# Differential attention: loads and operands of q and k earlier, and three small steps in other forms

## The chip, the cores and the metric

The kernel runs on one core of one Trainium2 chip. The metric is the time of one execution on the device in microseconds (us), the median of several runs. The names of the engines: TensorE (PE, with its weight loads shown as PEld), VectorE (DVE), ScalarE (ACT), GpSimd (POOL) and SyncE (SP), which here only issues transfers.

## What is computed

One step of a two-layer decoder trunk: a gated-linear-attention layer and a differential-attention layer, each followed by a squared-ReLU MLP and a post-LayerNorm. There is a prompt of 1024 tokens behind 16 meta tokens, and eight running sequences that read a paged cache of 4096 keys each. The change touches the differential attention of the prompt:

```python
def diff_core(q, k, v, q_pos, k_pos, lam):        # 8 heads, two maps m of width 64 each
    s = jnp.einsum('bqhmd,bkhmd->bhmqk', q, k).astype(F32) * (DIFF_DH ** -0.5)
    mask = k_pos[None, :] <= q_pos[:, None]
    s = jnp.where(mask, s, -jnp.inf)
    p = jax.nn.softmax(s, axis=-1)
    a = p[:, :, 0] - lam * p[:, :, 1]
    return jnp.einsum('bhqk,bkhe->bqhe', a, v.astype(F32))

def diff_output(o, g_sub, lam_init, w_out, dtype):
    o = rms_norm(o, g_sub) * (1.0 - lam_init)     # over the 128 values of a head
    return o.reshape(B, T, DIFF_HEADS * DIFF_DV).astype(dtype) @ w_out
```

q, k and v come from one projection of 1024 to 3072 columns, the first 16 of each 64 columns of q and k rotated. The k and v rows are outputs as well.

## The kernel before, in words

All data is float32. Large products take each operand as a high part (rounded) and a low part (the rest), and add three products: `mm3` (L186). `split` (L182) makes the two parts, the high one by a copy on ScalarE, the low one by a subtraction on VectorE.

The program is one function on one core, in stages one after the other: the first layer (to about 1450 us), the projections for q, k and v (to about 1775 us), the attention (to about 2075 us), and the output product and second MLP. A scheduler orders the instructions on each engine when the program is built: it goes by the order in the program text and by a simulated timeline, and `tc.issue_after(i)` keeps what stands in it behind instruction `i`. On the chip each engine works in that order and waits where an operand or a buffer isn't ready.

**Projections** (L1050). Twelve units of 256 columns: 0 to 3 give q, 4 to 7 k, 8 to 11 v. `kunit` loads a unit's weights (raw pieces in two buffers of `wrp`, high and low parts in two buffers each of `wsp`, named whi and wlo); GpSimd makes the low part (L175). A unit has four blocks of 256 tokens, each of 48 products (16 x three), a copy to SBUF (L1061), for q and k four small VectorE operations for the rotation, and a store (L1078) to `qd` or to the outputs. `next(paged)` puts a piece of the paged decode behind each block. The tokens' operands lie in XH and XL, two halves of 512 tokens each.

**Attention.** `prep(h)` (L1113) loads the k rows, q rows, 16 meta rows of k, and the values of head `h` back from memory, into two buffers each: k and q in wlo, values and meta rows of k in whi, meta rows of v in `vm`. TensorE transposes k and q into `axt` (three PSUM buffers), `split` makes the parts, in the half of XH and XL with the parity of `h`. For all heads but 0, nine transfers on GpSimd's queue (L1151 to L1157) then put the operands so that the high and low part of a map's k lie above each other in the 128 rows, and q's beside them: two products of full height give a score. Head 0 has no such transfers and uses three products of 64 rows (L1175 to L1177).

`tile_` (L1160) does 128 queries of one head. For each map and each piece of up to 512 keys: scores into `mmt` (three PSUM buffers), scale, mask and running minimum on VectorE (L1183); then the exponential with its sum on ScalarE (L1185), the factor of the second map (L1187, L1188), the combination of the maps (L1189), transposes on TensorE (L1198), copies on ScalarE (L1200), and the product with the values (L1203) into `po`. Five tiles can be in flight (`scp`). `prep(h + 1)` stands ahead of a head's first tile in the text.

Behind every fourth tile, `po` is copied to Y, squared as a whole on ScalarE (L1239), and summed by value rows on VectorE (L1240) into `oss`. For every two heads `o_norm` (L1207) makes the norm's factor, a power on GpSimd (L1214), and multiplies Y by it (L1215): on GpSimd for heads 0 to 6, on VectorE for head 7, whose two halves are followed by `o_fm`, which brings Y into XH and XL for the output product.

Of the kernel before, what the change touches and what calls it, by code (L numbers as in the profile page):

```python
# [11 lines left out]
F32 = mybir.dt.float32  # L12
# [99 lines left out]
def hybrid_step(ctx, tc, A, dbg=None, upto=9):  # L112
# [73 lines left out]
    def mm3(ps, ah, al, bh, bl, first, last):  # L186
        TE.matmul(ps, ah, bh, start=first, stop=False)  # L187
        TE.matmul(ps, ah, bl, start=False, stop=False)  # L188
        TE.matmul(ps, al, bh, start=False, stop=last)  # L189
# [860 lines left out]
    for u in range(12):  # L1050
        hi, lo = kunit(wd, u * 256)
        hv, lv = (x.rearrange("p (k n) -> p k n", n=256) for x in (hi, lo))
        for t2_ in range(4):
            ps = mmt()
            for i in range(2):
                t = 2 * t2_ + i
                a = slice(t * P, (t + 1) * P)
                for k in range(NB):
                    mm3(ps[:, i * 256 : (i + 1) * 256], XH[:, k, a], XL[:, k, a], hv[:, k, :], lv[:, k, :], k == 0, k == NB - 1)
            o = qt.tile([P, 2, 256], F32, name="qo")  # L1060
            S.copy(o.rearrange("p i n -> p (i n)"), ps)  # L1061
            rows = slice(2 * t2_ * P, (2 * t2_ + 2) * P)
            pr = slice(NM + rows.start, NM + rows.stop)
            if u < 8:
                tmp = qt.tile([P, 2, 4, 16], F32, name="qr")
                pv = ps.rearrange("p (i n d) -> p i n d", i=2, d=64)
                ov = o.rearrange("p i (n d) -> p i n d", d=64)
                tb = rtab[:, 2 * t2_ : 2 * t2_ + 2]
                V.tensor_tensor(ov[:, :, :, 0:16], pv[:, :, :, 0:16], bc(tb[:, :, 0:16], [P, 2, 4, 16], 2), op=ALU.mult)
                V.tensor_tensor(tmp[:, :, :, 0:8], pv[:, :, :, 8:16], bc(tb[:, :, 16:24], [P, 2, 4, 8], 2), op=ALU.mult)  # L1070
                V.tensor_tensor(tmp[:, :, :, 8:16], pv[:, :, :, 0:8], bc(tb[:, :, 24:32], [P, 2, 4, 8], 2), op=ALU.mult)
                steps_v.append(V.tensor_tensor(ov[:, :, :, 0:16], ov[:, :, :, 0:16], tmp, op=ALU.add).ins)
            if u < 4:
                dst = qd[rows, u * 256 : (u + 1) * 256]
            else:
# [12 lines left out]
        elif u == 3:  # L1088
            list(paged)
# [478 lines left out]
```

## Time and profile before

| | |
|---|---|
| median of 3 runs | 2875.54 us (2874.0 to 2877.55) |
| the profiled execution | 2875.13 us |
| its span, first to last instruction | 2873.2 us |
| mean granted TensorE clock | 0.983 |
| attention, 1777 to 2075 us: PE, DVE, ACT, POOL busy of 298 us | 268.67, 236.01, 198.15, 68.22 us |
| granted clock in that stretch | 0.93 |

Busy time is the time in which an engine works on instructions; a matmul's end is modelled, so that a busy TensorE is not one at its peak. The granted clock is the share of the full TensorE clock. In a row of a group stand the line, engine, operation, output and inputs, shapes and count, then the total busy time in us and the mean of one in ns, then the idle time before them with what ended it. A row of the timeline begins with its start and its duration in us. An arrow in brackets names what the engine waited for.

### The profile page before, as it was taken

The page shows a single profiled execution, that of the slowest core. Times are in us where ns is not written, and L with a number is a line of the kernel's source. Part 1 is how long each engine was busy: PE and PEld are TensorE (multiplying, and loading weights), DVE is VectorE, ACT ScalarE, POOL GpSimd, SP SyncE. Part 2 cuts the span into 40 slices and gives each one's busy share as a digit, 9 for nine tenths or more (in the row PEclk, how much of TensorE's full clock was granted, in tenths as well). Part 3 has the DMA queues.
Part 4 walks back from the last instruction along what each step waited for, and adds up shares of the span by engine and source line. Part 5 has one row for each costly group of instructions (what it writes and reads, how often), then busy time and mean ns, then how long its engine had stood idle before and what let it go on. Part 6 is the DMA issues. An engine that isn't in the chain of part 4 may idle for free. (4 is left out here: it accounts for less than half of the span.)

```text
span 2873.2 us, 52001 instructions
## 1 busy us (share of the span) xinstructions
PE 2757.3 (96%) x19653; PEld 2269.7 (79%) x19653; DVE 1974.9 (69%) x3048; ACT 1083.8 (38%) x2117; POOL 1148.1 (40%) x811
## 2 busy tenths in 40 slices
PE   8889999999999999999999999988999999999997
PEld 5666777997777777777798978878889888797985
DVE  2565544568887778777668711788638888978788
ACT  3233444252221221221331112677525536355553
POOL 1230212334343443433233321032236766777764
PEclk9899999999999999999999998899999999999999
DMA  7557741625798898888569984464334554554573
GB/s 249 180 187 257 250 175 41 245 91 170 282 339 305 319 353 307 322 323 303 198 233 317 363 327 137 89 144 98 118 99 89 114 131 107 136 122 113 128 188 89
DMA packets 276871, 577.28 MB, mean 201 GB/s; under 512 B 24567, under 2 KB 139837, under 8 KB 272525
## 3 DMA queue, kind: packets, MB, share of 16 engines
q1 hardware_dynamic: 252284, 520.66, 51.9%
q0 software_dynamic: 24336, 53.31, 10.7%
q8 instruction: 154, 2.52, 0.4%
q14 instruction: 97, 0.79, 0.1%
HBM read 531.16 MB, written 29.26 MB: 195 GB/s over the span
## 5 line engine op out<-in xcount | busy, mean ns | idle before, releaser
L175 POOL TENSOR_TENSOR wlo<-raw,whi 128x512 fp32r<-128x512 f32 x256 | 372.5, 1469 | 750.5 <-ACT whi L174 669.7
L187 PE MATMUL mmt<-whi,XH 128*128 128x256 f32 (+1 forms) x1760 | 524.5, 300 | 1.1 <-ACT Y L311 0.7
L188 PE MATMUL mmt<-wlo,XH 128*128 128x256 f32 (+1 forms) x1760 | 524.8, 299 | 0.6 <-POOL wlo L175 0.6
L187 PE MATMUL mmt<-XH,whi 128*128 128x512 f32 (+1 forms) x1216 | 436.0, 359 | 7.9 <-DVE HL L184 2.9
L189 PE MATMUL mmt<-whi,XL 128*128 128x256 f32 x1536 | 435.7, 285 | 0.1
L189 PE MATMUL mmt<-XH,wlo 128*128 128x512 f32 (+1 forms) x1216 | 432.2, 356 | 0.0
L174 ACT CAST whi<-raw 128x512 fp32r<-128x512 f32 x256 | 152.6, 619 | 584.1 <-PE mmt L189 181.9
L791 DVE TENSOR_REDUCE sc<-pg 128x16 f32<-128x1024 f32 x256 | 308.3, 1211 | 76.3 <-POOL pg L790 73.8
L188 PEld LDWEIGHTS mmt<-wlo,XH 128*128 128x128 f32 x1760 | 332.1, 189 | 29.0 <-issue 18.1
L187 PEld LDWEIGHTS mmt<-whi,XH 128*128 128x128 f32 x1760 | 331.1, 189 | 25.6 <-issue 11.8
L188 PE MATMUL mmt<-XL,whi 128*128 128x512 f32 x768 | 306.4, 399 | 0.0
L790 DVE TENSOR_TENSOR pg<-pg,qb 128x1024 f32<-128x1024 f32 x192 | 262.3, 1374 | 62.2 <-DMA pg<-in_cache_k 55.4
L189 PEld LDWEIGHTS mmt<-whi,XL 128*128 128x128 f32 x1536 | 289.7, 189 | 11.4 <-issue 10.1
L187 PEld LDWEIGHTS mmt<-XH,whi 128*128 128x128 f32 x1216 | 229.7, 189 | 55.5 <-issue 12.9
L790 POOL TENSOR_TENSOR pg<-pg,qb 128x1024 f32<-128x1024 f32 x64 | 162.3, 2538 | 252.1 <-DMA pg<-in_cache_k 182.6
L189 PEld LDWEIGHTS mmt<-XH,wlo 128*128 128x128 f32 x1216 | 229.8, 189 | 34.5 <-issue 2.1
L187 PE MATMUL mmt<-whi,HH 128*128 128x512 f32 x512 | 204.7, 401 | 4.6 <-DVE Y L1015 4.5
L189 PE MATMUL mmt<-whi,HL 128*128 128x512 f32 x512 | 203.9, 398 | 0.0
L188 PE MATMUL mmt<-wlo,HH 128*128 128x512 f32 x512 | 203.4, 397 | 0.0
L1413 POOL TENSOR_TENSOR wlo<-rw,whi 128x512 fp32r<-128x512 f32 x92 | 157.7, 1779 | 86.2 <-ACT whi L1412 67.7
L1413 POOL TENSOR_TENSOR wlo<-RW,whi 128x512 fp32r<-128x512 f32 x96 | 167.3, 1788 | 53.7 <-ACT whi L1412 53.7
L188 PEld LDWEIGHTS mmt<-XL,whi 128*128 128x128 f32 x768 | 144.9, 189 | 39.1 <-issue 7.9
(440 smaller groups left out, 5837.3 us busy)
## 6 DMA issues: line engine op xcount, KB each, us to landing
pg<-in_cache_k SPq DMA_DIRECT2D x256, 512.0 KB, 6.5
pg<-in_cache_v SPq DMA_DIRECT2D x256, 512.0 KB, 6.4
raw<-in_mlp_w SPq DMA_DIRECT2D x164, 256.0 KB, 4.6
swt<-in_mlp_w SPq DMA_DIRECT2D x32, 1024.0 KB, 5.0
rw<-in_mlp_w SPq DMA_DIRECT2D x116, 256.0 KB, 3.3
RW<-in_mlp_w POOLq DMA_DIRECT2D x96, 256.0 KB, 5.7
raw<-in_gla_w_in SPq DMA_DIRECT2D x48, 256.0 KB, 3.0
swt<-in_gla_w_in SPq DMA_DIRECT2D x12, 1024.0 KB, 4.9
```

What stands on the lines that cost most here:

```text
L174: S.copy(hi[:, c], raw)
L175: G.tensor_tensor(lo[:, c], raw, hi[:, c].bitcast(F32), op=ALU.subtract)
L187: TE.matmul(ps, ah, bh, start=first, stop=False)
L188: TE.matmul(ps, ah, bl, start=False, stop=False)
L189: TE.matmul(ps, al, bh, start=False, stop=last)
L790: eng.tensor_tensor(pg, pg, qb, op=ALU.mult)
L791: return V.tensor_reduce(sc[:, n, :], pg.rearrange("p (h d) -> p h d", d=64), op=ALU.add, axis=AX.X).ins
L1413: G.tensor_tensor(lo[:, k, :], t, hi[:, k, :].bitcast(F32), op=ALU.subtract)
```

## The change

- The rows of q and k, and the meta rows of k, get a pool of their own (`rqp`, two buffers each). `load_qk(h)` loads them. Heads 0 and 1 are loaded behind unit 9's blocks in the projections, head `h + 2` at the sixth tile of head `h`. Values are loaded by `load_v`, at the fourth tile of the head before.
- `prep` has two parts: first the transposes, parts and moves of k, then those of q, a tile later. Head 0 gets the nine moves too, so that all heads use two products of 128 rows; its three-product form is gone.
- Head 0's `prep` is done amid the projections. For that, units 10 and 11 are interleaved: first the blocks that read tokens 0 to 511 (and block 2 of unit 10), then three blocks of the second half; `prep(0)` writes the first half of XH and XL and stands behind the first product of block 1 of unit 11.
- The factor of the second map (L1188) is a scalar_tensor_tensor with one pointer scalar instead of a tensor_scalar with two.
- `o_norm` multiplies Y on VectorE for all heads, in pieces of 512 columns.
- The sums of squares are made by ScalarE: four squares of 128 columns with an accumulated sum each, instead of one square of 512 and a reduction on VectorE.

```diff
+    er = ExitStack()
+    rqp = er.enter_context(tc.tile_pool(name="rqp", bufs=2, side="right"))
+    def load_qk(h):
+        raw = rqp.tile([P, 2, 8, P], F32, name="rqk")
+        km = rqp.tile([NM, P], F32, name="rkm")
+        kr = A["k_rows_p"][0, 0, :, h, :]
+        dma(km, kr[:NM])
+        dma(raw[:, 0], kr[NM:].rearrange("(t p) d -> p t d", p=P))
+        dma(raw[:, 1], qd[:, h * P : (h + 1) * P].rearrange("(t p) d -> p t d", p=P))
+        return raw, km
+
+    def prep(h, raw, km):
...
+        for c in range(2):
+            ps = axt()
+            for i in range(4):
+                TE.transpose(ps[:, i * P : (i + 1) * P], kx[:, 4 * c + i, :], ident)
+            cs = slice(NM + 512 * c, NM + 512 * c + 512)
+            split(kh_[:, cs], kl_[:, cs], ps)
+        move(k2[1][64:], kh_[64:])
+        move(kh_[64:], kl_[:64])
+        move(k2[1][:64], kl_[64:])
+        yield k2, q2, ql2
...
+        for a, b in (q2, ql2):
+            move(b[64:], a[64:])
+            move(b[:64], a[64:])
+            move(a[64:], a[:64])
+        yield
+
+    units, outs = {}, []
+    blocks = [(u, t) for u in range(10) for t in range(4)]
+    blocks += [(10, 0), (10, 1), (10, 2), (11, 0), (11, 1), (10, 3), (11, 2), (11, 3)]
+    for u, t2_ in blocks:
+        if t2_ == 0:
+            units[u] = [x.rearrange("p (k n) -> p k n", n=256) for x in kunit(wd, u * 256)]
+        if (u, t2_) == (10, 3):
+            nxt = prep(0, *raws[0])
+            with tc.issue_after(outs[-2 * NB]):
+                head = next(nxt)
+                next(nxt)
...
+        elif (u, t2_) == (9, 3):
+            raws = [load_qk(0), load_qk(1)]
...
-                if h == 0:
-                    TE.matmul(ps, q2[r, ts_], k2[r, x:y], start=True, stop=False)
-                    TE.matmul(ps, q2[r, ts_], kl_[r, x:y], start=False, stop=False)
-                    TE.matmul(ps, ql2[r, ts_], k2[r, x:y], start=False, stop=True)
-                else:
-                    TE.matmul(ps, q2[m][:, ts_], k2[m][:, x:y], start=True, stop=False)
-                    TE.matmul(ps, ql2[m][:, ts_], k2[m][:, x:y], start=False, stop=True)
+                TE.matmul(ps, q2[m][:, ts_], k2[m][:, x:y], start=True, stop=False)
+                TE.matmul(ps, ql2[m][:, ts_], k2[m][:, x:y], start=False, stop=True)
...
-        V.tensor_scalar(neg[:, 0:1], neg[:, 1:2], l[:, 0:1], lamv[:, 1:2], ALU.mult, ALU.mult)
+        V.scalar_tensor_tensor(neg[:, 0:1], neg[:, 1:2], lamv[:, 1:2], l[:, 0:1], ALU.mult, ALU.mult)
...
-        eng.tensor_tensor(Yd[:, ts, hs], Yd[:, ts, hs], bc(r, [P, n, m, P], 3), op=ALU.mult)
+        for x in range(0, n, 4 // m if n > 4 else n):
+            a = slice(ts.start + x, ts.start + x + (4 // m if n > 4 else n))
+            V.tensor_tensor(Yd[:, a, hs], Yd[:, a, hs], bc(r[:, a.start - ts.start : a.stop - ts.start], [P, a.stop - a.start, m, P], 3), op=ALU.mult)
...
+    vnxt = load_v(0)
     for h in range(8):
-        head = nxt
+        if h:
+            head = hnxt
+        vh = vnxt
         for n, t in enumerate((3, 2, 1, 0, 7, 6, 5, 4) if h == 7 else (7, 1, 5, 3, 6, 0, 4, 2)):
-            if n == 0 and h < 7:
-                nxt = prep(h + 1)
+            if h < 7:
+                if n == 0:
+                    nxt = prep(h + 1, *raws[h + 1])
+                    hnxt = next(nxt)
+                elif n == 1:
+                    next(nxt)
+                elif n == 3:
+                    vnxt = load_v(h + 1)
+                elif n == 5 and h < 6:
+                    raws.append(load_qk(h + 2))
...
-                S.activation(po, po, AF.Square)
-                V.tensor_reduce(oss[:, ts, h], po.rearrange("p (t e) -> p t e", e=P), op=ALU.add, axis=AX.X)
+                for i in range(4):
+                    x = po[:, i * P : (i + 1) * P]
+                    j = ts.start + i * (ts.step or 1)
+                    S.activation(x, x, AF.Square, accum_out=oss[:, j, h : h + 1])
```

144 lines of the change are left out of this document (59 added, 85 removed).

## The prediction

> **What bounds the kernel now.** I read the page's head first, then busy time by head of the attention stage, then what waits at the stage's start and at the change of heads, then the groups that the change touches. The page has TensorE (PE) as the busiest engine by far:
>
> ```profile
> span 2873.2 us, 52001 instructions
> PE 2757.3 (96%) x19653; PEld 2269.7 (79%) x19653; DVE 1974.9 (69%) x3048; ACT 1083.8 (38%) x2117; POOL 1148.1 (40%) x811
> ```
>
> Outside attention the projections keep PE full. All edits lie in attention, from about 1775 to 2075 us, so it is read alone. The next rows cut it where a head's last value product ends (after the bounds: length, then PE, PEld, DVE, ACT, POOL busy with counts, granted clock, DMA share, GB/s).
>
> ```profile
> 1777.00:1826.00 49.00, 45.27 (x262) 38.80 (x262) 33.23 (x112) 27.27 (x64) 4.85 (x9) 0.76 0.53 123
> 1826.00:1860.00 34.00, 28.87 (x203) 26.51 (x201) 24.71 (x84) 21.56 (x51) 4.59 (x9) 0.90 0.55 118
> 1860.00:1891.00 31.00, 26.87 (x199) 23.71 (x198) 27.07 (x77) 21.10 (x54) 11.23 (x11) 1.00 0.62 129
> 1891.00:1923.00 32.00, 29.95 (x214) 27.46 (x213) 28.28 (x98) 24.53 (x58) 4.59 (x9) 0.95 0.60 125
> 1923.00:1956.00 33.00, 27.96 (x198) 24.76 (x197) 28.57 (x81) 22.59 (x55) 11.19 (x11) 0.95 0.52 121
> 1956.00:1988.00 32.00, 30.08 (x217) 27.83 (x216) 28.11 (x100) 24.99 (x63) 4.59 (x9) 0.95 0.41 93
> 1988.00:2021.00 33.00, 29.18 (x211) 26.53 (x209) 28.89 (x87) 22.96 (x57) 11.14 (x11) 0.95 0.41 90
> 2021.00:2075.00 54.00, 50.50 (x398) 46.83 (x398) 37.15 (x95) 33.13 (x69) 16.05 (x12) 1.00 0.34 111
> ```
>
> From 1860 to 2021 (161 us) VectorE (DVE) is busy 140.9, or 87%, PE 144.0, or 89%, ScalarE (ACT) 116.2, or 72%. No engine is full: PE and DVE pass tiles to each other, and a stall of either costs. Head 0 takes 49 us where the five heads from 1860 take 32.2 on average, 17 more. Its start:
>
> ```profile
> 1774.58 0.27 PE L189 MATMUL mmt<-whi,XL 128*128 128x256 f32 x1
> 1778.34 0.42 PE L1175 MATMUL mmt<-XH 64*128 64x352 f32 x1 [0.68 <-ACT XH L183]
> 1782.23 0.26 PE L1135 MATMUL axt<-c_ident,whi 16*128 16x16 f32 x1 [2.21 <-DMA whi<-out_k_rows_p]
> ...
> 1780.00:1782.00 2.00, 0.02 (x1) 0.00 (x0) 0.00 (x0) 0.00 (x0) 0.00 (x0) 0.64 1.14 342
> 1782.00:1784.00 2.00, 1.77 (x9) 1.75 (x9) 1.52 (x6) 0.60 (x2) 0.00 (x0) 0.50 1.19 291
> 1800.00:1804.00 4.00, 4.00 (x19) 3.61 (x18) 2.32 (x7) 1.31 (x3) 0.51 (x1) 0.50 0.85 152
> ```
>
> The last projection starts at 1774.58, head 0's first score at 1778.34; then PE, in order, stands 2.21 us at head 1's transpose for the 16 meta rows, and from there runs at half clock (0.50) until 1804. Head 2 has the other visible stall:
>
> ```profile
> 1831.01 0.51 POOL L1151 DMA_DIRECT2D XH<-XH  x1 [27.91 <-ACT XH L183]
> 1846.93 0.51 POOL L1157 DMA_DIRECT2D XL<-XL  x1 [4.67 <-DMA XL<-XL]
> 1847.10 0.40 PE L1179 MATMUL mmt<-XH 128*128 128x352 f32 x1 [2.68 <-DMA XH<-XH]
> 1849.79 0.66 PE L1180 MATMUL mmt<-XH,XL 128*128 128x352 f32 x1 [1.19 <-DMA XL<-XL]
> 1850.49 0.52 DVE L1183 CUSTOM_DVE_ANT_0 as<-mmt,cmask 128x352 f32<-128x352 f32 x1 [3.83 <-PE mmt L1180]
> ```
>
> Its operands' moves run from 1831.01 until 1849.79 (18.8 us), and PE wants them 3.9 us earlier (2.68 and 1.19).
>
> **The change, part by part.** Rows for the costs, all from the groups and lines of attention but the two of L688, which are the same operation in the GLA layer:
>
> ```profile
> L1188 DVE TENSOR_SCALAR ast<-ast,ls,lamv 128x1 f32<-128x1 f32 x64 | 17.2, 270 | 0.7
> L1212 DVE SCALAR_TENSOR_TENSOR orr<-ls x6: 139/168/177, 1846.5 to 2044.0; 128x16 f32<-128x16 f32 x3, 128x4 f32<-128x4 f32 x2, 128x8 f32<-128x8 f32 x1
> L1240 DVE TENSOR_REDUCE oss<-smt 128x4 f32<-128x512 f32 x16 | 11.0, 686 | 0.0
> L1239 ACT ACTIVATE smt<-smt 128x512 f32<-128x512 f32 x16 | 9.4, 590 | 0.1
> L688 ACT ACTIVATE axt<-axt x32: 368/380/382, 162.5 to 478.5; 128x256 f32<-128x256 f32 x32
> L688 ACT ACTIVATION_READ_ACCUMULATOR axt<-axt x32: 184/188/191, 162.8 to 478.8; 128x1 f32 x32
> L1189 DVE SCALAR_TENSOR_TENSOR as<-as,ast 128x528 f32<-128x528 f32 x8 | 18.3, 2290 | 0.1
> 2021.02 0.77 DVE L1189 SCALAR_TENSOR_TENSOR as<-as,ast 128x528 f32<-128x528 f32 x1
> 2000.19 4.74 DVE L1189 SCALAR_TENSOR_TENSOR as<-as,ast 128x528 f32<-128x528 f32 x1
> 2000.70 3.66 POOL L1215 TENSOR_TENSOR Y<-Y,orr 128x2048 f32<-128x2048 f32 x1
> L1215 DVE TENSOR_TENSOR Y<-Y,orr x2: 680/1230/1781, 2044.2 to 2070.5; 128x512 f32<-128x512 f32 x2
> ```
>
> *DVE.* The factor (L1188) becomes one scalar_tensor_tensor: 64 x (0.270 - 0.150, near the small ones of L1212) = -7.7; ends 0 and -8.4 (at 0.139). The reduction (L1240) goes: -11.0. The norm's row leaves POOL. While POOL runs it for 3.66 us, DVE's combination of the maps takes 4.74 instead of 0.77; the group's 18.3 us less five at 0.77 leaves 14.4 for three, an excess of 12.1: -12.1. The same rows come back on DVE as 14 pieces of 128x512 (four for each of three pairs of heads, two for head 6) at 0.68: +9.5, or 24.9 if all met POOL as the 1.781 one may have. Sum: -21.3 us of DVE. What of it is time: nothing, if PE at 89% is what limits; all, if DVE is. The three stalls hold both engines up, the rest is spread, so I take two thirds: **-14**, ends 0 and -21 (and +2 if the pieces cost 24.9 and the factor nothing).
>
> *ACT.* Sixteen squares of 128x512 become 64 of 128x128 with their accumulator reads. From 0.380 at 256 and 0.590 at 512 columns follows an estimate of 0.275 at 128: 64 x (0.275 + 0.188) - 9.4 = +20.2 us busy, 2.5 for a head. Behind them on ACT wait the next exponentials and the copies that free transposes. ACT is idle some 9 of 32 us in a head, which is the cover: **+2**, ends 0 and +20. [...]
>
> *Head 0.* Its third term goes, 28 matmuls; at the spacing below of 0.16 for such a one (1778.92 - 1778.76, full clock), or twice that at half clock, 4.5 to 9 us of PE. Its loads, transposes, casts and nine POOL moves go among the last blocks, where these rows show the cover:
>
> ```profile
> 1750.00:1765.00 15.00, 15.00 (x130) 15.00 (x129) 0.00 (x0) 1.76 (x3) 0.00 (x0) 1.00 0.48 141
> 1769.28 0.59 ACT L1061 COPY qo<-mmt 128x512 f32<-128x512 f32 x1 [5.12 <-PE mmt L189]
> 1774.93 0.59 ACT L1061 COPY qo<-mmt 128x512 f32<-128x512 f32 x1 [5.07 <-PE mmt L189]
> 1741.75 1.29 POOL L175 TENSOR_TENSOR wlo<-raw,whi 128x512 fp32r<-128x512 f32 x1 [2.32 <-ACT whi L174]
> 1778.76 0.32 PE L1175 MATMUL mmt<-XH 64*128 64x352 f32 x1
> 1778.92 0.32 PE L1176 MATMUL mmt<-XL,XH 64*128 64x352 f32 x1
> 1817.27 0.41 PE L1179 MATMUL mmt<-XH 128*128 128x352 f32 x1
> 1826.27 0.33 SPq L1125 DMA_DIRECT2D whi<-out_k_rows_p  x1
> ```
>
> DVE and POOL idle there wholly, ACT nearly. A block lasts 1774.93 - 1769.28 = 5.65 us; three follow the last one that reads the tokens' first half, 17 us, and PE's transposes for head 0, which with their waits now fill 1774.9 to 1778.3, add up to 3.4. A chain of moves took 18.8 and starts behind the first casts, by an estimate half of those 3.4 in: ready 0 to 4 us after PE is free. New is also that nothing of head 1 waits for meta rows then. Ends: nothing gained, or all 17 us of the excess. A first head must still fill the pipeline through mask, exponential, combination and transposition, so I take **-7**, nearer the third term's price than the whole excess.
>
> *Heads 1 to 7.* q and k rows come from a pool of their own and no longer wait, as the meta rows in the value buffer do, for the values of the head before last. The number of moves is the same. They start when the head before last has its last score, up to 9 us earlier by the rows above (head 1's first score at 1817.27, so head 0's last are done; meta rows for head 2 asked for only at 1826.27). Head 2's 3.9 us go, with DVE's 3.83 lying mostly under them: **-4**, ends 0 and -8 (a half-speed clock follows there). Late next would be value rows, which still wait for their buffer.
>
> *Loads and order of blocks.* Each head's five loads become three for q and k and two for values, the same bytes. Those of heads 0 and 1 pass unit 10's and 11's weights on SP. Unit 11 is wanted one block sooner, at 1774.93 - 5 x 5.65 = 1746.7, and its last low part ended at 1743.0: 3.7 us to spare. If the loads (two heads x 2 x 1024 rows x 512 bytes, 2.1 MB, 6 us at the 342 GB/s above) delay it wholly, PE stands 2.3: **+1**, ends 0 and +6.
>
> *Sum.* -14 + 2 - 7 - 4 + 1 = -22. The profiled execution took 2875.13 us (1.9 beyond its span; the median of the runs is 2875.54): 2875.1 - 22 = **2853**.
>
> **The rivals.**
> *DVE's time is worth nothing,* as PE sets the pace (89% against 87%): only starts gain, 2875 + 2 - 7 - 4 + 1 - 3 (a quarter of the three stalls, which stop PE too) = 2864. Against it: DVE's waits and PE's alternate.
> *All comes through:* DVE's full -21, head 0 -14, head 2 -4, ACT +2, loads +1: 2839. For it: the half clock from 1782 to 1804 alone costs head 0 up to half of 22 us, and follows a stall that goes. [...]
> *Head 0's moves come late and nothing else but the stalls gains:* head 0 gets 0, DVE a quarter (-5), head 2 -4, ACT +4, loads +2: 2872, no measurable change.
> *ScalarE becomes what is waited for, slower:* at every fourth tile four squares with reads, 1.85 us in place of 0.59, stand ahead of the next exponentials, DVE then has no tile to combine, and its saved time is idleness. Price 16 x 1.26 = 20; with DVE's gain 0, head 0 and 2 -7 and -4, loads +1: 2885. It decides when over 10 us of the 20 show and DVE gives nothing. For it: in the last stretch ACT is busy 33 of 54, and most DVE waits pass through it; against: 72% busy.
>
> **How the numbers follow.** Measurable here is about 0.2%, 5.75 us. Chances: forecast 0.38 (2845 to 2861 its own range), 2864 0.22, 2839 0.15, 2872 0.08, 2885 0.17. Faster: 0.75; same: 0.08; slower: 0.17. The range 2835 to 2880 leaves out most of the slower case and the lower tail of 2839, some 0.18.
>
> **What would show it.** Right: no 4.7 us combinations on DVE; the stretch from the last projection to head 0's last value product near 42 instead of 49 us; heads of about 30; no PE wait on a move at head 2; ACT some 20 us busier. Wrong: DVE or PE idle before ScalarE's squares, PE idle at head 0's first score with the clock at 0.5 as long as before, PE waiting for unit 11's weights, or the idle time of DVE growing by what it saved.

## The result, and the profile after

The changed kernel takes 2879.73 us (median of 14 runs, 2871.69 to 2888.9). The kernel before, run beside it, takes 2877.48 us (2871.14 to 2886.32). The ratio is 1.0002, with a 95% interval of 0.9991 to 1.0013: no difference that can be measured, where 2853 us was forecast. The profiled execution took 2880.64 us.

The head of the page, and then the attention stage as a whole, from the copy of the last projection to the start of the last norm row. The two windows are taken from the two traces between the same events (bounds, length, then PE, PEld, DVE, ACT, POOL busy, clock, DMA share, GB/s). After:

```profile
span 2878.9 us, 52057 instructions
PE 2751.6 (96%) x19625; PEld 2273.8 (79%) x19625; DVE 1944.6 (68%) x3046; ACT 1093.9 (38%) x2229; POOL 1146.8 (40%) x816
...
1787.50:2083.50 296.00, 257.88 (x1820) 239.19 (x1820) 214.04 (x717) 205.29 (x570) 55.07 (x78) 0.92 0.49 112
```

Before:

```profile
1774.90:2070.50 295.60, 266.47 (x1865) 240.08 (x1866) 232.60 (x724) 198.59 (x463) 66.97 (x81) 0.92 0.48 112
```

VectorE does 18.6 us less, TensorE 8.6 us less, ScalarE 6.7 us more, and the stage takes as long as before (296.0 against 295.6). The work went, and idle time came in its place. By head, cut as before where a head's values are done:

```profile
1787.00:1834.00 47.00, 36.06 (x233) 32.26 (x232) 29.68 (x104) 27.17 (x71) 5.10 (x10) 0.89 0.49 113
1834.00:1868.00 34.00, 30.20 (x209) 27.94 (x208) 24.97 (x90) 24.27 (x70) 4.58 (x9) 0.90 0.54 118
1868.00:1902.00 34.00, 29.14 (x204) 26.39 (x204) 26.24 (x88) 24.33 (x69) 7.54 (x10) 0.95 0.58 117
1902.00:1937.00 35.00, 30.42 (x216) 28.73 (x215) 25.31 (x91) 24.34 (x70) 4.58 (x9) 0.90 0.54 115
1937.00:1970.00 33.00, 28.74 (x203) 26.04 (x201) 25.36 (x88) 24.47 (x70) 7.55 (x10) 0.95 0.56 121
1970.00:2000.00 30.00, 28.64 (x216) 26.63 (x214) 28.03 (x100) 25.68 (x73) 4.58 (x9) 1.00 0.45 98
2000.00:2034.00 34.00, 29.48 (x221) 27.94 (x219) 26.35 (x96) 25.24 (x78) 7.83 (x11) 0.90 0.56 125
2034.00:2088.00 54.00, 49.54 (x373) 47.26 (x372) 32.44 (x74) 31.36 (x77) 14.57 (x11) 0.91 0.37 111
```

Head 0 is shorter and at a higher clock (47 us at 0.89, before 49 at 0.76). The heads behind it are not shorter: 30 to 35 us where 30 were forecast and 31 to 34 stood before, at 0.90 to 0.95 in six of the last seven rows, where the rows from 1860 before had 0.95 to 1.00.

What TensorE waited for in the stage, from the table of waits (us in total, times, the longest; the largest entries). After:

```profile
PE mmt L1192 <- DMA XL<-XL: 9.4, 7, 2.8
PE mmt L1191 <- issue: 9.2, 3, 3.5
PE mmt L1191 <- DVE ast L1195: 7.7, 7, 2.0
PE mmt L1191 <- DMA XH<-XH: 6.0, 2, 3.8
PE axt L1210 <- DVE as L1201: 1.7, 3, 0.8
```

Before:

```profile
PE axt L1198 <- DVE as L1189: 7.1, 5, 3.5
PE axt L1135 <- DMA whi<-out_k_rows_p: 4.3, 4, 2.2
PE mmt L1179 <- DMA XH<-XH: 2.7, 1, 2.7
```

L1191 and L1192 are the scores. The three "issue" waits begin and end while the last moves of a head are under way, so I count them with the others: 24.6 us in which scores wait for moves, 5.0 of them at head 0's start and 19.6 spread over all seven changes of heads. Before, it was 3.9 us at one change (2.7 above and the 1.19 us quoted with head 2). In exchange the waits for the combination (L1189, now L1201) and for the meta rows are nearly gone. One such place, at the change to head 7, in the timelines of TensorE, VectorE and GpSimd:

```profile
2020.71 0.78 PE L1191 MATMUL mmt<-XH 128*128 128x272 f32 x2 [3.82 <-DMA XH<-XH]
...
2018.29 0.90 DVE L1201 SCALAR_TENSOR_TENSOR as<-as,ast 128x656 f32<-128x656 f32 x1
2023.69 0.44 DVE L1195 CUSTOM_DVE_ANT_0 as<-mmt,cmask 128x272 f32<-128x272 f32 x1 [4.50 <-PE mmt L1192]
...
2017.81 0.52 POOL L1095 DMA_DIRECT2D XH<-XH  x1 [5.60 <-issue]
```

TensorE comes to head 7's first score at 2016.9, and the eighth of nine moves is only issued at 2017.81. It stands 3.82 us. At 2019.19 VectorE has combined a tile of head 6, whose transposes and value products TensorE could do, but they stand behind the score in its order; then VectorE has nothing left and idles 4.50 us. The clock is at 0.50 from 2020.7 to 2024.8. Another of the twelve waits is one of 3.34 us that ends at 1922.53, with the clock at 0.50 behind it:

```profile
1920.00:1922.50 2.50, 0.00 (x0) 0.00 (x0) 0.00 (x0) 2.16 (x7) 0.64 (x2) 1.00 0.52 108
1922.50:1925.00 2.50, 1.28 (x3) 0.93 (x4) 0.00 (x0) 0.00 (x0) 0.00 (x0) 0.51 0.53 105
1925.00:1927.50 2.50, 2.50 (x14) 2.50 (x12) 1.28 (x6) 0.00 (x0) 0.00 (x0) 0.50 0.00 0
1927.50:1929.50 2.00, 2.00 (x11) 2.00 (x10) 1.16 (x7) 0.93 (x2) 0.00 (x0) 0.53 0.00 0
1929.50:1935.00 5.50, 5.50 (x46) 5.35 (x45) 3.86 (x15) 4.49 (x14) 0.00 (x0) 1.00 0.02 4
```

Why is TensorE there so early? The scheduler chose the place. This is the share of a head's value products that stand ahead of the next head's first score, counted in TensorE's order in the two traces:

```
change of heads       0-1   1-2   2-3   3-4   4-5   5-6   6-7
before                0.64  0.55  0.86  0.64  0.77  0.55  0.77
after                 0.55  0.55  0.55  0.55  0.55  0.55  0.55
```

The moves, in turn, hardly come earlier. Counted from the end of the value products of the head before last, the first of a head's nine moves is issued 1.4 to 1.6 us behind it for heads 2 to 7 (4.8 to 6.5 before), but from the first issue to the last, called the chain below, go 14.2 to 18.6 us (12.5 to 15.9 before). So the last one is issued 15.7 to 20.0 us behind that point, where it was 18.6 to 21.5.

### The profile page after: what moved, and what is told of

The parts are those of the page before. It is cut to its first block, busy times and chain, and to the rows that moved or that the text cites. A ratio compares the mean times of both kernels' runs of the same rounds, so it can differ in the third digit from the quotient of the medians.

```text
span 2878.9 us, 52057 instructions
## 1 busy us (share of the span) xinstructions
PE 2751.6 (96%) x19625; PEld 2273.8 (79%) x19625; DVE 1944.6 (68%) x3046; ACT 1093.9 (38%) x2229; POOL 1146.8 (40%) x816
## 3 DMA queue, kind: packets, MB, share of 16 engines
q0 software_dynamic: 25056, 55.69, 11.2%
## 5 line engine op out<-in xcount | busy, mean ns | idle before, releaser
L187 PEld LDWEIGHTS mmt<-whi,XH 128*128 128x128 f32 x1760 | 332.6, 190 | 27.9 <-issue 12.2
L189 PEld LDWEIGHTS mmt<-whi,XL 128*128 128x128 f32 x1536 | 291.5, 190 | 8.8 <-issue 8.0
L187 PEld LDWEIGHTS mmt<-XH,whi 128*128 128x128 f32 x1216 | 229.5, 189 | 53.3 <-issue 12.9
```

The source lines that it names most:

```text
L189: return TE.matmul(ps, al, bh, start=False, stop=last)
```

## The experiments

The ratios are to the kernel before, run on the same chip in the same session; in brackets the 95% interval. "Attention" is the stage as above in the profiled execution, "waits" the time that scores wait for moves in it. For orientation: before 295.6 and 3.9 us, after 296.0 and 24.6.

**The two halves of the change.** `e1_loads_only` is the changed kernel with the three small edits undone:

```diff
-V.scalar_tensor_tensor(neg[:, 0:1], neg[:, 1:2], lamv[:, 1:2], l[:, 0:1], ALU.mult, ALU.mult)
+V.tensor_scalar(neg[:, 0:1], neg[:, 1:2], l[:, 0:1], lamv[:, 1:2], ALU.mult, ALU.mult)
...
-    V.tensor_tensor(Yd[:, a, hs], ...
+    G.tensor_tensor(Yd[:, ts, hs], ...
...
-for i in range(4):
...
-    S.activation(x, x, AF.Square, accum_out=oss[:, j, h : h + 1])
+S.activation(po, po, AF.Square)
+V.tensor_reduce(oss[:, ts, h], po.rearrange("p (t e) -> p t e", e=P), op=ALU.add, axis=AX.X)
```

(The norm's row goes back to GpSimd for heads 0 to 6 and stays on VectorE for head 7. Code is cut at each "...".)

> The loads, the two-part operands and head 0 as in the changed kernel; the factor, the norm's row and the squares as before. Theory 'moves' (TensorE reaches a head's first score before that head's nine transfers have landed, and what VectorE saves turns into this wait): VectorE's three combinations of 4.7 us come back, so the next head's scores are asked for later at heads 3 and 7 and wait less there; in sum within 5 us of the kernel before and of the changed one. Rival 'ScalarE' (the 64 small squares cost what the rest gains): 10 us or more faster than the changed kernel. Rival 'worthless' (VectorE's time is no time at all): within 3 us of the changed kernel.

`e2_small_only` is the kernel before with these lines the other way round.

> The factor, the norm's row and the squares as in the changed kernel; loads, operands and head 0 as before. Theory 'moves': TensorE's order puts every head's first score at 0.55 of the head before, but the transfers start only when that head starts, so TensorE waits for them at six or seven heads, some 5 us each instead of 3.9 at one: 5 to 20 us slower than the kernel before, although VectorE is less busy by some 18 us. Rival 'ScalarE': slower by 5 to 15 us, with VectorE waiting for exponentials and not TensorE for transfers. Rival 'worthless': within 3 us of the kernel before.

Measured: loads only 2872.97 us, 0.9975 (0.9961 to 0.9990), attention 286.6, waits 15.3. Small edits only 2874.08 us, 0.9992 (0.9975 to 1.0009), attention 291.5, waits 13.5. So the loads alone gain a little, the small edits alone nothing that can be measured, and both together nothing: they don't add up, and each half alone already has 13 to 15 us of waits on moves. The theory "moves" had e2 5 to 20 us slower than the kernel before, which it is not, in spite of these waits. The first scores stand at 0.55 at five of the seven changes in both, so either half alone moves the order: the shorter work of VectorE is not needed for it.

**The moves.** `e3_whole_prep` makes q's operands directly behind k's, nine moves in one piece, at the first tile:

```diff
-        move(k2[1][64:], kh_[64:])
...
-        yield k2, q2, ql2
...
+        move(k2[1][64:], kh_[64:])
...
+        yield k2, q2, ql2
...
-                elif n == 1:
-                    next(nxt)
```

> The changed kernel with the operands made in one piece: k's and q's transposes together at the head's first tile and then all nine transfers, as in the kernel before. Theory 'moves': q's transfers are issued 3 to 4 us sooner, TensorE's waits for transfers (some 26 us over eight heads) fall by half, and the time by 8 to 15 us. Rivals 'ScalarE' and 'worthless': within 3 us of the changed kernel.

`e4_no_moves_2to7`:

```diff
+        if h < 2:
+            move(k2[1][64:], kh_[64:])
...
-        for a, b in (q2, ql2):
+        for a, b in (q2, ql2) if h < 2 else ():
```

> The changed kernel with no transfers of operands for heads 2 to 7, whose scores are then made of what lies there: part of the computation is left out. Theory 'moves': the waits at heads 2 to 7 (some 17 us) and the half-speed clock behind them go; 15 to 25 us faster than the changed kernel. Rivals 'ScalarE' and 'worthless': at most 4 us faster (the transfers' issues on GpSimd were nobody's wait).

Measured: e3 2866.36 us, 0.9962 (0.9946 to 0.9977), attention 276.9, waits 12.7; e4 2844.5 us, 0.9882 (0.9857 to 0.9907), attention 258.7, waits 8.6, all of heads 0 and 1. e3 takes 13 us off with the first scores still at 0.55 at five changes and at 0.64 at two, so q's place a tile behind k's has a price of its own. Without the moves the kernel is 34 to 35 us faster (by ratio or by medians), more than the 15 to 25 expected and far more than the 16.0 by which the waits fall. ScalarE and VectorE have the same work there, so it isn't their work that keeps the changed kernel at its time. What of the 34 us is the moves' lateness and what their load on the DMA engines and on GpSimd, this run doesn't tell. The same 140 us in the middle, after and e4:

```profile
1860.00:2000.00 140.00, 124.93 (x888) 115.63 (x888) 111.11 (x386) 104.78 (x296) 24.25 (x38) 0.95 0.50 107
```

```profile
1860.00:2000.00 140.00, 134.78 (x1026) 126.17 (x1025) 127.72 (x451) 121.12 (x348) 9.15 (x5) 1.00 0.18 50
```

Without moves TensorE is 96% busy at full clock and VectorE 91%; with them 89% and 79%.

`e5_moves_sorted` takes e3 and issues first the six moves that only read what the casts wrote, then the three that overwrite a half.

> The kernel of e3_whole_prep with its nine moves in another order: first the six that only read what the casts wrote, then the three that overwrite a half which an earlier move reads. GpSimd, in order, then no longer waits at the second, sixth and ninth move for the landing of the one before. Theory moves (what the matrix engine waits for is the landing of the last move): the chain per head shortens from 12 to 21 us to about 9 to 14, the engine's waits on moves fall from 12.7 us to under 8, and the time from 2866 to 2858 to 2864 (ratio about 0.994). Theory that the chain's length is set by the transfers themselves and not by the order of issue: chain and time as in e3_whole_prep, within 3 us.

Measured: 2864.88 us, 0.9955 (0.9938 to 0.9972), chains 12.6 to 18.6 us for heads 2 to 7, waits 13.7. As e3: the order of issue is not what sets the chain. `e10_moves_sp` asks the same of the issuing engine (on e8, below):

```diff
-        move = nc.gpsimd.dma_start
+        def move(a, b):
+            if h:
+                nc.sync.dma_start(a.bitcast(F32), b.bitcast(F32))
+            else:
+                nc.gpsimd.dma_start(a, b)
```

> The kernel of e8_norm_pool with the moves of heads 1 to 7 issued by SP's queue in place of GpSimd's (the same bytes, taken as plain f32). Order of the matrix engine's work as in e8_norm_pool. Theory moves with GpSimd as the price (issue of 0.5 us each, in order, behind the power and the norm's row): the chain from first to last move falls from 11 to 20 us to under 10, the engine's waits on moves for heads 2 to 7 (11 us in e8_norm_pool) to under 4, the time from 2855 to 2840 to 2850. Theory that the transfers' own time is the price: chain and time as in e8_norm_pool, within 3 us. If the loads behind them on SP come late: slower than 2858, with waits on the value rows.

Measured: 2856.97 us, 0.9917 (0.9889 to 0.9945), against 0.9930 of e8: no difference. The first and the last move of head 2, and the window between them:

```profile
1826.63 0.51 SPq L1074 DMA_DIRECT2D XH<-XH  x1
1843.02 0.46 SPq L1074 DMA_DIRECT2D XL<-XL  x1
```

```profile
1827.00:1843.00 16.00, 14.01 (x109) 12.96 (x109) 14.80 (x51) 13.42 (x37) 0.00 (x0) 1.00 0.91 202
```

The chain is 16.4 us long here too (16.3 for head 2 in e8), with GpSimd out of it, and the 16 DMA engines are 91% busy on average. So `e18_no_qk_loads` takes other transfers away, the loads of q and k rows that fall into the same time:

```diff
                 elif n == 5 and h < 6:
-                    raws.append(load_qk(h + 2))
+                    raws.append(raws[h])
```

> The changed kernel without the loads of q and k rows for heads 2 to 7: their operands are made from the rows of heads 0 and 1 again, so their scores are those of other heads (left out are six times three loads, 1.05 MB a head; all other work, the moves too, is as in the changed kernel). Theory shared transfers (the loads fall into the same 17 us as the nine moves, in which the 16 DMA engines are 0.95 busy, and so make the moves late): the chains of heads 2 to 7 fall from 14 to 19 us to 11 to 14, the waits on moves from 24.6 us to under 14, the time to 2864 to 2872. Theory that the chain is set by the moves alone (issue, landing, the next one behind it): chains within 2 us, time 2876 to 2882.

Measured: 2850.72 us, 0.9897 (0.9870 to 0.9923), attention 268.5, waits 11.2; chains of heads 2 to 6 from 17.1, 18.6, 17.7, 17.9, 14.2 us to 13.5, 16.4, 13.4, 15.3, 13.4, only head 7's stayed long (17.9 and 19.1). The issues with the median time to landing in the last column, after and e18:

```profile
XH<-XH POOLq DMA_DIRECT2D x24, 256.0 KB, 6.2
XL<-XL POOLq DMA_DIRECT2D x24, 256.0 KB, 7.2
```

```profile
XH<-XH POOLq DMA_DIRECT2D x24, 256.0 KB, 3.5
XL<-XL POOLq DMA_DIRECT2D x24, 256.0 KB, 4.4
```

Same moves, same queue, same order of issue: a move of 256 KB lands in 3.5 to 4.4 us where it took 6.2 to 7.2. The direction is that of shared transfers. The gain of 29 us is more than the 8 to 16 expected, and more than the 13.4 us by which the waits fall; where the rest comes from isn't shown. In the kernel before, these loads lie beside the moves as well: the rows of head 5 are asked for at 1866.51 and 1866.94, and the moves of head 3 start at 1866.73. The changed kernel asks for the rows of head 5 at 1874.8, and its moves of head 3 start at 1869.83. So the rows of head 5 were asked for 63 us ahead of that head's first move before (1929.2), and are so now (1938.3): the scheduler had already put these loads two heads ahead.

**The place of the first scores.** `e14_scores_held` is the changed kernel with one edge for the scheduler, and no move is touched:

```diff
-            tile_(h, t, po[:, at * P : (at + 1) * P], *vh, *head)
+            with tc.issue_after(held) if h and n == 0 else nullcontext():
+                last = tile_(h, t, po[:, at * P : (at + 1) * P], *vh, *head)
+            if n == 4:
+                held = last                       # last value product of the fifth tile
```

> The changed kernel with one edge more: the matrix engine's work of a head's first tile is ordered behind the value products of the fifth tile of the head before, so that a first score comes after 0.73 of that head's value products in place of 0.55. Nothing else is changed, and no move is earlier. Theory order (the engine, in order, stands at scores whose moves have not landed, and all work behind it with it): waits on moves of heads 1 to 7 fall from 20 us to under 8, the time to 2862 to 2872. Theory that the moves' lateness itself is the price, not the place of the scores: waits fall but as much idle time comes elsewhere, 2876 to 2882. Theory that the order was good as it was: slower than 2882.

`e16_scores_held_late` has `n == 6` there, `e15_whole_held` the edge in e8, `e17_before_held` the edge in the kernel before.

> As e14_scores_held, but the first tile is held behind the seventh tile's value products (0.91 of the head before), by when the moves have landed with some 8 us to spare. Theory order: no waits on moves for heads 1 to 7, but the vector engine runs out of masks at each change of heads, 2 to 4 us each: slower than e14_scores_held by 5 to 20 us. Theory that the place of the scores does not matter: as e14_scores_held.

> The kernel of e8_norm_pool (operands in one piece, norm's row on GpSimd) with the same edge as e14_scores_held. Theory order: its waits on moves of heads 2 to 7 (11 us) fall to under 4 and the time from 2855 to 2846 to 2852. Theory that its moves land early enough already and the later place costs cover: 2855 to 2862.

> The kernel before the change with the edge of e14_scores_held: a first score comes after 0.73 of the value products of the head before (before the change its places were 0.55 to 0.86). With the order alike in both, the difference to e14_scores_held is what the change's edits are worth. Theory that the edits gain once the order is right: 2872 to 2880 here, 8 to 16 us behind e14_scores_held's 2863.7. Theory that the edge is all the gain and the edits are worth nothing: 2860 to 2868.

Measured (the edge is a lower bound: in e17 two changes, 4-5 and 6-7, have 0.91):

| | us | ratio | attention | waits |
|---|---|---|---|---|
| after (places 0.55) | 2879.73 | 1.0002 (0.9991 to 1.0013) | 296.0 | 24.6 |
| e14 (0.73) | 2863.66 | 0.9954 (0.9937 to 0.9972) | 277.3 | 10.4 |
| e16 (0.91) | 2866.79 | 0.9964 (0.9945 to 0.9982) | 278.1 | 2.0 |
| e15 (e8 with 0.73) | 2855.97 | 0.9929 (0.9906 to 0.9952) | 272.1 | 8.7 |
| e17 (before with 0.73) | 2879.5 | 1.0017 (1.0001 to 1.0033) | 290.2 | 1.2 |

TensorE's waits on moves in e14, and the group of masks on VectorE in the changed kernel and in e14 (idle time before them in the last column):

```profile
PE mmt L1192 <- DMA XL<-XL: 5.8, 6, 3.2
PE mmt L1191 <- DMA XH<-XH: 4.6, 2, 2.7
```

```profile
L1195 DVE CUSTOM_DVE_ANT_0 as<-mmt,cmask 128x272 f32<-128x272 f32 (+5 forms) x128 | 62.0, 495 | 39.1 <-PE mmt L1192 38.5
```

```profile
L1195 DVE CUSTOM_DVE_ANT_0 as<-mmt,cmask 128x272 f32<-128x272 f32 (+5 forms) x128 | 61.8, 496 | 24.9 <-PE mmt L1192 24.1
```

And the largest wait of TensorE in e16:

```profile
PE mmt L1191 <- DVE ast L1195: 10.5, 21, 2.7
```

The edge alone takes 16 us off the changed kernel: the waits fall by 14.2 (for heads 1 to 7 from 19.6 to 5.3, under 8 as expected), VectorE's wait for scores by 14. In the kernel before it gains nothing. So the edge is no gain of its own; as I read it, it sets free what the edits had saved. With the same edge in both, the change is worth 2863.66 against 2879.5, some 16 us, and 12.9 us of attention by the two profiles. e16 shows the other side: of the waits on moves for heads 1 to 7 only 0.15 us is left, but it isn't faster than e14, nor slower by the 5 to 20 us expected; TensorE waits there for the masks that free a score's buffer (10.5 us, in e14 4.1). e15 shows it once more: the edge takes the waits for heads 1 to 7 from 11.1 us (e8) to 2.2, and the time stays (2855.97 against 2855.48), where 2846 to 2852 was one of the two expectations; TensorE's waits for the combination grow from 1.6 to 5.2 us. So a wait on a move that goes is not time by itself. It is in the changed kernel, where one edge brings both down.

**Head 0.** `e6_head0_old` is e3 with head 0 as before: transposes after the projections, three products of 64 rows, no moves.

> The kernel of e3_whole_prep with head 0 as before the change: its transposes after the last projection, scores from three products of 64 rows, no moves for head 0; the loads stay early. Theory moves: head 0's new form gains little, since its first scores wait for moves too and the projections got 3 us longer; undoing it costs 0 to 5 us against e3_whole_prep (2866 to 2871). By the prediction's term (head 0: -7): 2873. If head 0's moves and the reordered blocks cost more than they gain: below 2866.

Measured: 2866.27 us against e3's 2866.36. In the profiles attention is 7.1 us longer (284.0 against 276.9) and the projections 8.0 shorter (319.1 against 327.1). The two profiled executions lie at opposite ends of their runs (2871.22 the slowest of five, 2857.08 the fastest of ten), but the projections show a cause. Only 2.1 of the 8.0 us are head 0's transposes (their block is shown in the next section). Another 3.6 us are waits of TensorE for the low part of a unit's weights, which e6 and the kernel before don't have, and e3 and the changed kernel do. The longer one, 3.15 us in both, in unit 9's first block of the changed kernel:

```profile
1712.30 0.58 PE L188 MATMUL mmt<-wlo,XH 128*128 128x256 f32 x1 [3.15 <-POOL wlo L175]
...
1710.67 0.34 POOL L1167 MEMSET vm<- 128x128 f32 x2 [9.10 <-SPq L757]
1710.98 1.26 POOL L175 TENSOR_TENSOR wlo<-raw,whi 128x512 fp32r<-128x512 f32 x1
```

GpSimd, in its order, makes that low part behind two memsets of `vm` and stands 9.10 us before them; TensorE waits 3.15 us, and its clock is at 0.50 from 1710.9 to 1717.7. The order of GpSimd's work was made anew as well. So head 0's new form gains in the one stage, and what is lost in the other comes for the larger part from that place in GpSimd's order: an estimate of 5.5 us of the 8.0 in e3, if it is there as in the changed kernel. That is the 3.15 us, and 2.3 of the 5.4 us in which TensorE works at 0.50 behind them (1712.3 to 1717.7): its products start 0.21 us apart there, and 0.12 us apart at 0.99 behind that. What head 0's form would be worth without it, no run shows.

**Squares and norm.** `e7_square_one` and `e13_after_square_one` undo the squares in e3 and in the changed kernel. `e8_norm_pool` and `e9_after_norm_pool` put the norm's row back on GpSimd in the same two. `e11_q_norm_old` undoes both in e3; `e12_norm_spread` leaves the row on VectorE, but one piece ahead of each of four tiles.

> The kernel of e3_whole_prep with the squares as before the change: one square of 128x512 on the scalar engine and a reduction on the vector engine. Busy time: scalar engine -20, vector engine +11. Theory moves: within 3 us of e3_whole_prep (2863 to 2869), as both engines have room. Theory ScalarE (the small squares hold the next exponentials): 10 to 15 us faster than e3_whole_prep (2851 to 2856). Theory that the vector engine's time counts in full: some 8 us slower (2874).

> The changed kernel with the squares undone: one square of 128x512 on the scalar engine and a reduction on the vector engine; rows two heads ahead, q's piece apart, factor and norm's row stay. Theory ScalarE (in the changed kernel the small squares stand between k's casts and the exponentials, and cost what the loads' move gained; loads alone gave 2873): 6 to 12 us faster than the changed kernel, 2868 to 2874. Theory order (the scores are asked for ahead of their moves, whatever the squares): within 3 us of it, 2877 to 2882, waits on moves near 20 us.

> The kernel of e3_whole_prep with the norm's row of two heads back on GpSimd in one operation of 128x2048 (the two last half-head rows stay on the vector engine). The combinations on the vector engine that meet it should take about 4.7 us again, and the moves queued behind it on GpSimd start up to 3.7 us later. Vector engine: +12 -9.5 busy. Theory moves: 3 to 8 us slower than e3_whole_prep (2869 to 2874), by the stalls and by the later moves. Theory that the vector engine's time is worth nothing and the moves are hidden: within 2 us of it.

> The changed kernel with one part undone: the norm's row of two heads goes back to GpSimd, in one operation of 128x2048 (the two half-head rows at the end stay on the vector engine). Theory norm (in the changed kernel the row's four pieces stand in one burst of 2.5 us on the vector engine, which also waits there for GpSimd's power, itself behind moves; that gives back what the split of the stalls saved): 7 to 12 us faster than the changed kernel (2868 to 2873), attention 286 to 289 us. Theory moves (the null comes from scores asked for ahead of their moves, and nothing else): 0 to 3 us from the changed kernel, waits on moves still near 24 us. By the prediction's terms (stalls -12.1, pieces +9.5, two thirds of it time): 2 us slower.

> The kernel of e8_norm_pool with the squares undone too: one square of 128x512 on the scalar engine, reduction on the vector engine. Of the three small edits only the maps' factor is left. Theory that the squares cost or gain nothing, as between e3_whole_prep and e7_square_one (2866.4 and 2865.2): within 3 us of e8_norm_pool's 2855.5. Theory that with the norm off the vector engine its time is short elsewhere and the scalar engine's reads show: 4 to 8 us faster. Theory that the vector engine limits now: 4 to 8 us slower.

> The kernel of e3_whole_prep with the norm's row still in four pieces on the vector engine, but one ahead of each of four tiles of the next head instead of all four in a burst behind the power. Busy time as in e3_whole_prep. Theory norm as a burst (a wait of 1 to 2.5 us for the power plus 2.5 us in which no mask is applied, so the matrix engine runs dry): most of the 11 us between e3_whole_prep and e8_norm_pool comes back, 2855 to 2860. Theory norm as busy time (9.7 us on the vector engine count wherever they stand): within 3 us of e3_whole_prep, 2863 to 2869.

| | us | ratio | attention | waits |
|---|---|---|---|---|
| e7 (e3, squares old) | 2865.2 | 0.9956 (0.9940 to 0.9972) | 276.9 | 17.0 |
| e13 (after, squares old) | 2881.84 | 1.0008 (0.9991 to 1.0025) | 295.6 | 22.0 |
| e8 (e3, norm old) | 2855.48 | 0.9930 (0.9909 to 0.9950) | 271.8 | 15.6 |
| e9 (after, norm old) | 2879.67 | 0.9997 (0.9985 to 1.0010) | 290.4 | 16.3 |
| e11 (e3, both old) | 2868.3 | 0.9974 (0.9945 to 1.0003) | 275.9 | 13.7 |
| e12 (e3, norm spread) | 2860.26 | 0.9917 (0.9887 to 0.9948) | 283.7 | 15.0 |

The squares cost nothing in e3 and in the changed kernel: the theory that ScalarE is what is waited for falls. The norm's row on VectorE costs some 10 us in e3 (by medians of two sessions; the intervals, 0.9946 to 0.9977 and 0.9909 to 0.9950, just meet) and nothing in the changed kernel; no run shows why it differs. e8 and e9 are misses: e8 was expected 3 to 8 us slower than e3 and is 11 faster, and e9 has the expected time, but waits of 16.3 us where some 24 were expected: 8 us less of waits and no time. e12 can't be told from e8 (four runs, 2853.28 to 2873.89, the profiled one the slowest), so whether the burst or the busy time is the price is left open. e11 is a miss: with the norm off VectorE the old squares cost some 13 us by the medians (the intervals just meet), though they cost none in e7. I have no proven cause for that; each variant is scheduled anew, and the places of its first scores differ. The fastest kernels that leave nothing out are e8, e10 and e15, at 2855 to 2857 us, 0.7 to 0.8% below the kernel before; among them the runs don't decide.

## Why the prediction was wrong, step by step

**What bounds the kernel: right.** "PE and DVE pass tiles to each other, and a stall of either costs." The changed kernel shows what I didn't draw from it: time saved on one is worth something only if the other comes to its work in the right order.

**VectorE, -14: the work went, the time did not.** Groups of the changed kernel:

```profile
L1200 DVE SCALAR_TENSOR_TENSOR ast<-ast,lamv,ls 128x1 f32<-128x1 f32 x64 | 14.3, 223 | 0.7
L1229 DVE TENSOR_TENSOR Y<-Y,orr 128x512 f32<-128x512 f32 x16 | 12.2, 812 | 4.3 <-POOL orr L1226 4.3
L1201 DVE SCALAR_TENSOR_TENSOR as<-as,ast 128x528 f32<-128x528 f32 x8 | 6.1, 764 | 0.1
L1266 ACT ACTIVATE smt<-smt 128x128 f32<-128x128 f32 x64 | 17.4, 272 | 0.6
L1266 ACT ACTIVATION_READ_ACCUMULATOR smt<-smt 128x1 f32 x64 | 12.4, 194 | 0.0
```

The stalled combinations are gone (18.3 to 6.1 us, -12.2; forecast -12.1), the reduction too (-11.0), and the norm's pieces cost what was forecast (12.2 for sixteen, in place of 2.5 for two). The factor was mis-sized: 223 ns and not the 150 taken from L1212, so -2.9 and not -7.7. A wait was missed: the pieces stand behind GpSimd's power, itself among the moves, and VectorE waits 4.3 us for it. In sum these are 16.4 us less where 21.3 was forecast; the stage's 18.6 also hold 2.3 us of head 0's low parts, which are now made in the projections. I took two thirds of it for time, and its value was 0: the small edits alone (e2) gain nothing, and the loads alone (e1, 2872.97) are not slower than the whole change (2879.73). With the edge in both kernels (e14 against e17) all edits together are worth 16 us, where the sum was -22.

**ScalarE, +2: the time right, the work too high.** The two groups above add up to 17.4 + 12.4 us, which less the 9.4 before is 20.4, where 20.2 was forecast. But a square and its accumulator read overlap in the records: the 64 pairs keep ScalarE busy for 24.5 us, 383 ns a pair, 15.1 us more than before. Between e7 and e3, which differ in the squares alone, ScalarE's busy time in the stage differs by 9.4 us (193.7 and 203.1). So "ACT some 20 us busier" did not come; undoing the squares brings no time in e7 and e13. The size of one square was estimated well (272 ns, forecast 275, for a quarter of the 590 ns square's columns), that of a read too (194 ns, forecast 188).

**Head 0, -7: it came in one stage and went in the other.** I counted its transposes in TensorE's order there, but gave the longer projections no price, and TensorE is what the projections wait for (busy for all 42 us from 1745 to 1787). The copy behind the block with the transposes, in the changed kernel:

```profile
1768.35 0.59 ACT L1117 COPY qo<-mmt 128x512 f32<-128x512 f32 x1 [5.08 <-PE mmt L189]
1776.09 0.59 ACT L1117 COPY qo<-mmt 128x512 f32<-128x512 f32 x1 [2.18 <-PE mmt L189]
...
1790.77 0.56 PE L1191 MATMUL mmt<-XH 128*128 128x352 f32 x2 [2.17 <-DMA XH<-XH]
1794.12 0.95 PE L1192 MATMUL mmt<-XH,XL 128*128 128x352 f32 x2 [2.79 <-DMA XL<-XL]
```

That block lasts 7.74 us in place of 5.65, 2.1 more. And "ready 0 to 4 us after PE is free" was too early: its last operand is there at 1794.12, 6.6 us after the last copy at 1787.5. From the first move (1770.44) until then went 23.7 us, not the 18.8 taken from head 2. By e6 against e3 the whole form is worth nothing in time, where 7 us were forecast.

**Heads 1 to 7, -4: the step that failed.** "q and k rows ... no longer wait", "They start ... up to 9 us earlier", "Late next would be value rows." The meta rows' wait did go and the value rows were never late. But late next were the moves, at all seven changes of heads, 19.6 us in place of 3.9 at one (and 5.0 at head 0). They start only 3 to 5 us earlier, the last of them 3 us earlier at most (for head 7 a us later), and the scores are asked for at 0.55. Two things that I had in view and didn't carry through: the text puts q's six moves a tile behind k's (e3 undoes that and is 13 us faster), and the order of TensorE is made anew by a scheduler that, as the places show, asks for the next head earlier (e14 undoes that and is 16 us faster). That its timeline has the moves landing sooner than the chip does is what I conclude from e14, not something a run shows by itself.

**Loads and order of blocks, +1.** Unit 11's weights were in time and no row waits for them. But the low part of unit 9's was not: 3.15 us of TensorE's time and the half clock behind it, as shown with head 0. With the 2.1 us of head 0's transposes that is more than the 3.0 us by which the projections grew (from 322.9 to 325.9); where they gained in exchange stays open.

**The rivals.** The 2872 case ("no measurable change") named the right outcome and head 0's late moves, but not the later heads. In the 2864 case VectorE's time was worth nothing as TensorE sets the pace; here it was worth nothing as TensorE stood still. e14 gives back 16 us for all edits together; how much of that is VectorE's work, no run shows. The 2885 case is refuted by e13. Of the signs named against the forecast, "the idle time of DVE growing by what it saved" is there. "PE idle at head 0's first score" is there in part: it is idle for 5.0 us, but the clock is at 0.50 for some 7 us (1792.9 to 1799.6), and not for some 22 as before (1782 to 1804).

## What to carry to other kernels

When a program is scheduled at build time, a change of durations or of the text can move the order on an engine that it doesn't touch, as with the first scores in e2 (0.55 at five of the seven changes of heads, before at two): before pricing saved work, ask what the in-order engine will be told to do earlier, and whether its operands are there. Put a head's (or tile's) first use behind work that is surely ready by one explicit edge, and measure the edge with and without the edits, since alone each may show nothing. Read the time and not only the waits: in e15 and e16 waits went and no time with them. Look for the new order on the helping engines too, as with GpSimd's memsets here. Count the transfers that share the DMA engines with those on the critical path: here a move of 256 KB landed some 2.7 us later with the loads beside it (6.2 and 7.2 us, in e18 3.5 and 4.4).

## What the runs showed of the hardware that was not expected

- Moves from SBUF to SBUF, half of the partitions each, keep the 16 DMA engines 0.95 busy at 191 GB/s together with the loads (1869.8 to 1889 of the changed kernel), and at 0.91 for 202 GB/s when SP issues them (1827 to 1843 of e10). In the projections a share of 1.03 went with 370 GB/s:

```profile
1869.80:1889.00 19.20, 16.21 (x115) 13.88 (x114) 16.56 (x54) 13.56 (x38) 7.54 (x10) 1.00 0.95 191
...
1600.00:1700.00 100.00, 99.59 (x926) 89.40 (x925) 54.48 (x86) 17.59 (x32) 25.20 (x18) 1.00 1.03 370
```

- In the windows shown with the result, the clock is at 0.50 behind one wait of 3.34 us, and it is back at 1.00 by 1929.5, 7.0 us after the wait ended, with 1.19 us more of waiting in between. From 1924.36, where the work became continuous, that took 5.1 us. Another such stretch has no single wait of that length ahead of it: behind waits of 0.90 and 1.62 us, which end at 1889.25 and 1891.27, the changed kernel's clock is at 0.50 from 1891.8 to 1895.2.
- What the norm's row on GpSimd cost VectorE differed with the instruction that met it. In e8, with the row on GpSimd again, no combination of 528 keys is stalled (767 ns in the mean, 2290 before), and one small norm operation (at 1998.10, beside a row from 1997.84) takes 3400 ns where the others of its line take 148 to 169:

```profile
L1222 DVE SCALAR_TENSOR_TENSOR orr<-ls 128x8 f32<-128x8 f32 x1 | 3.4, 3400 | 0.0
L1199 DVE SCALAR_TENSOR_TENSOR as<-as,ast 128x528 f32<-128x528 f32 x8 | 6.1, 767 | 0.0
```

In e9, the changed kernel with the same row, three of the four rows stall VectorE again, now on the factor (4.57, 4.58 and 2.70 us for one of 128x1). Its group takes 26.5 us where it took 14.3:

```profile
L1200 DVE SCALAR_TENSOR_TENSOR ast<-ast,lamv,ls 128x1 f32<-128x1 f32 x64 | 26.5, 413 | 0.7
```

So the 12.1 us of stalls are not lost to the row on GpSimd as such: some 12 us in e9 too, some 3 in e8. How much it was differed between these orders of the program.
